# The sparse layer's mixer with projections written transposed

## The chip, the cores and the metric

One core of a Trainium2 chip runs the whole forward pass of a small two-layer trunk on 256 tokens of width 1024, batch 1, in float32. What counts is the device time of one execution in microseconds. A core has TensorE (PE), VectorE (DVE), ScalarE (ACT), GpSimd (POOL) and SyncE (SP), which here only issues transfers. Data lie in SBUF, TensorE writes PSUM, weights come from HBM.

## What is computed

Layer 0 has a mixer of a convolution and latent attention, layer 1 the sparse mixer that is changed here, and each has an MLP behind it. In the sparse mixer 16 heads in 4 groups look at keys in three ways: 15 compressed blocks, selected blocks (with 256 tokens all are selected, so it is causal attention with a slope) and a window. Gates weigh the three.

```python
proj = xn @ w_in          # q 1024 | k_c v_c k_s v_s k_w v_w, 256 each | gates 48
blk = z[:, idx] + pe      # 15 blocks of 32 tokens, starts 16 apart
kc = gelu(einsum('bnlgd,lde->bnge', blk_k, w1_k)) @ w2_k      # vc likewise
o_cmp = softmax(q kc' * scale - slope * dist) * has @ vc
o_slc = softmax(q k_s' * scale - slope * dist) @ v_s
o_win = softmax(q k_w' * scale - slope * dist) @ v_w
out = (g0 * o_cmp + g1 * o_slc + g2 * o_win) @ w_out
x = x + rms_norm(out, gain)
```

## The kernel before

Tokens are two tiles of 128 (`t`), the width is 8 slices of 128. Each product with weights is exact to nearly float32: weights and inputs are split into a high and a low part, and `mm3` (L112) adds three matmuls. A weight chunk (`chunk`, L156) is one transfer of 512 KB on SP into one of 4 raw buffers, two copies of 128x512 on ScalarE (`whi`) and two subtractions on VectorE (`wlo`); 5 slots hold them, 3 more (`x`) hold chunks that are loaded ahead for the next stage.

There are two forms of projection. Straight (`group_steps`, L202): the tokens are stationary and 512 (or 304, 256) weight columns move, tokens come out on partitions. Turned (`hidden_steps`, L346, in the MLPs): 128 weight columns are stationary and both token tiles move, 256 columns, outputs come out on partitions.

The order on TensorE is written out by hand. `mm` and `tr` add planned ns to a clock (`tick`), `defer(ns, fn)` puts a step off until the clock has passed, `need` runs steps until a condition holds, and `fill(ns)` in the head loop spends credit on pieces of other projections. The other engines' orders are made by the framework's scheduler from priorities.

The sparse mixer (`mixer_c`, L675) before: `c_in` group 0 (compressed inputs k_c, v_c) and group 1 (keys) straight, then v_s with gates, then queries of heads 0 to 7. What comes out on token rows is transposed by TensorE: tokens for the compression (`tok`, L650), split keys (L770), split queries (`q8`, L828). `compress` (L657) multiplies 16 slices onto 64 rows. In the head loop each of 32 head tiles has scores (`sc`) in two matmuls, then score reduction on VectorE (L921), exponential on ScalarE (L923), scaling by sum and gate on GpSimd (L928), and 5 heads later (`LAG`) a transposition of the probabilities (`pbn` to `pt`, L947). Eight heads make a unit; its compressed scores go through `cmp_scores` (`cs`, `cpc`, `ptc`), and its product with the values is given out piece by piece (`pv`). Remaining v_w, queries 8 to 15 and the output projection are the filling. `finish` (L275) ends a layer half: norm, update of X, transposition of the new X.

## Time and profile before

| | us |
|---|---|
| median of 3 runs (lowest, highest) | 645.55 (644.36, 645.79) |
| the profiled execution, its span | 644.01, 641.9 |
| TensorE, VectorE, ScalarE, GpSimd busy | 626.1, 418.2, 379.7, 78.0 |
| sparse mixer, first projection matmul to first MLP matmul | 307.37 to 454.87 |

Records of TensorE overlap, since matmuls are pipelined: 128x512 is shown with some 0.39 us though the next starts 0.23 us later. The price of an instruction is the time between starts, taken from a timeline, not its record.

### The profile page before, as it was taken

The page shows a single profiled execution, that of the slowest core. Times are in us where ns is not written, and L with a number is a line of the kernel's source. Part 1 is how long each engine was busy: PE and PEld are TensorE (multiplying, and loading weights), DVE is VectorE, ACT ScalarE, POOL GpSimd, SP SyncE. Part 2 cuts the span into 40 slices and gives each one's busy share as a digit, 9 for nine tenths or more (in the row PEclk, how much of TensorE's full clock was granted, in tenths as well). Part 3 has the DMA queues.
Part 4 walks back from the last instruction along what each step waited for, and adds up shares of the span by engine and source line. Part 5 has one row for each costly group of instructions (what it writes and reads, how often), then busy time and mean ns, then how long its engine had stood idle before and what let it go on. Part 6 is the DMA issues. An engine that isn't in the chain of part 4 may idle for free.

```text
span 641.9 us, 10332 instructions
## 1 busy us (share of the span) xinstructions
PE 626.1 (98%) x3630; PEld 532.5 (83%) x3630; DVE 418.2 (65%) x971; ACT 379.7 (59%) x866; POOL 78.0 (12%) x135
## 2 busy tenths in 40 slices
PE   7999999999999999999999999989999999999995
PEld 4889877889999988888889886666789999888884
DVE  6668797766666744446847787763966675644443
ACT  4886566756655644446727678875855565544431
POOL 1212330020000000000200055550300000000000
PEclk9999999999999999999999999999999999999999
DMA  8867335645555566556614825121646646556621
GB/s 270 293 184 219 124 106 198 222 138 196 192 178 188 185 205 198 194 185 244 213 34 136 290 99 165 33 67 58 210 149 209 198 166 201 191 197 195 197 68 65
DMA packets 32611, 110.09 MB, mean 172 GB/s; under 512 B 4080, under 2 KB 4656, under 8 KB 32560
## 3 DMA queue, kind: packets, MB, share of 16 engines
q1 hardware_dynamic: 32560, 109.44, 51.7%
q8 instruction: 28, 0.46, 0.3%
q14 instruction: 23, 0.19, 0.1%
HBM read 108.38 MB, written 1.05 MB: 170 GB/s over the span
## 4 chain that ended last, share of the span: by engine, by line
PE 63%; issue 28%; DVE 4%; ACT 2%; DMA 2%; POOL 1%; SPq 0%; DVEq 0%; POOLq 0%; ACTq 0%
PE acc L93 52%; PE sc L93 5%; PE tr L100 4%; DMA X<-in_x 1%; PE tr L105 1%; DMA raw<-in_a_in 1%; DVE wlo L172 1%; DVE xtl L255 1%; PE yp L93 1%; ACT pbn L923 1%; DVE X L293 1%; POOL rp L140 0%; ACT sq L270 0%; DVE xlo L172 0%; DVE pst L283 0%
## 5 line engine op out<-in xcount | busy, mean ns | idle before, releaser
L172 DVE TENSOR_TENSOR wlo<-raw,whi 128x512 fp32r<-128x512 f32 (+3 forms) x368 | 236.4, 681 | 123.3 <-ACT whi L171 121.3
L171 ACT ACTIVATE whi<-raw 128x512 fp32r<-128x512 f32 (+3 forms) x362 | 205.8, 614 | 135.5 <-PE acc L93 89.0
L93 PE MATMUL acc<-xtl,whi 128*128 128x256 f32 x384 | 107.9, 281 | 0.0
L93 PE MATMUL acc<-xth,wlo 128*128 128x256 f32 x384 | 107.5, 280 | 0.0
L93 PE MATMUL acc<-xth,whi 128*128 128x256 f32 x384 | 107.5, 280 | 0.0
L93 PE MATMUL acc<-whi,hl 128*128 128x512 f32 x256 | 99.8, 390 | 0.0
L93 PE MATMUL acc<-whi,hh 128*128 128x512 f32 x256 | 99.6, 389 | 0.0
L93 PE MATMUL acc<-wlo,hh 128*128 128x512 f32 x256 | 99.6, 389 | 0.0
L93 PE MATMUL acc<-whi,xth 128*128 128x512 f32 (+3 forms) x224 | 85.6, 382 | 1.1 <-DVE whi L167 1.1
L93 PE MATMUL acc<-wlo,xth 128*128 128x512 f32 (+3 forms) x224 | 84.4, 378 | 1.2 <-DVE wlo L172 1.0
L93 PE MATMUL acc<-whi,xtl 128*128 128x512 f32 (+3 forms) x224 | 85.2, 380 | 0.0
L93 PEld LDWEIGHTS acc<-xth,wlo 128*128 128x128 f32 x384 | 72.6, 189 | 0.0
L93 PEld LDWEIGHTS acc<-xth,whi 128*128 128x128 f32 x384 | 72.1, 188 | 0.1
L93 PEld LDWEIGHTS acc<-xtl,whi 128*128 128x128 f32 x384 | 72.1, 188 | 0.1
L93 PEld LDWEIGHTS acc<-whi,hh 128*128 128x128 f32 x256 | 48.1, 188 | 9.9
L93 PEld LDWEIGHTS acc<-wlo,hh 128*128 128x128 f32 x256 | 48.1, 188 | 9.9
L93 PEld LDWEIGHTS acc<-whi,hl 128*128 128x128 f32 x256 | 48.1, 188 | 9.9
L140 POOL TENSOR_TENSOR rp<-mse,mhalf 128x1 f32<-128x1 f32 x8 | 4.8, 596 | 395.4 <-DVE mse L137 395.4
L93 PEld LDWEIGHTS acc<-whi,xth 128*128 128x128 f32 x224 | 42.2, 188 | 10.3 <-issue 2.8
L93 PEld LDWEIGHTS acc<-wlo,xth 128*128 128x128 f32 x224 | 42.0, 188 | 8.8 <-DVE wlo L172 2.5
L93 PEld LDWEIGHTS acc<-whi,xtl 128*128 128x128 f32 x224 | 42.1, 188 | 6.6
L928 POOL TENSOR_SCALAR pbn<-pbn,sm,gates 128x128 f32<-128x128 f32 (+1 forms) x64 | 37.7, 600 | 75.1 <-DVE sm L925 72.7
(249 smaller groups left out, 883.4 us busy)
## 6 DMA issues: line engine op xcount, KB each, us to landing
raw<-in_w SPq DMA_DIRECT2D x128, 512.0 KB, 4.0
raw<-in_c_in SPq DMA_DIRECT2D x16, 512.0 KB, 3.7
raw<-in_a_in SPq DMA_DIRECT2D x15, 512.0 KB, 4.6
raw<-in_a_out SPq DMA_DIRECT2D x8, 512.0 KB, 3.7
raw<-in_c_out SPq DMA_DIRECT2D x8, 512.0 KB, 3.3
raw<-in_a_qup SPq DMA_DIRECT2D x6, 384.0 KB, 3.5
gpost<-in_gpost SPq DMA_DIRECT2D x4, 512.0 KB, 5.0
bias<-in_bias SPq DMA_DIRECT2D x4, 512.0 KB, 5.2
```

Of the source, the lines that this page charges most:

```text
L93: self.nc.tensor.matmul(ps, a, b, start=start, stop=stop, **({"skip_group_check": True} if part else {}))
L100: self.nc.tensor.transpose(dst, src, self.ident)
L105: self.nc.tensor.transpose(dst.bitcast(F32R), src, self.ident_r)
L140: nc.gpsimd.tensor_tensor(r, e, self.mhalf, op=OP.pow)
L171: nc.scalar.activation(hi[:, sl], raw[:, sl], AF.Copy)
L172: nc.vector.tensor_tensor(lo[:, sl], raw[:, sl], hi[:, sl].bitcast(F32), op=OP.subtract)
L255: nc.vector.scalar_tensor_tensor(lo, src, gcol, hi.bitcast(F32), OP.mult, OP.subtract)
L293: nc.vector.scalar_tensor_tensor(self.X[t][:, sl], self.tmp.pop(0), r, self.X[t][:, sl], OP.mult, OP.add)
L923: nc.scalar.activation(pb[:, sl], pb[:, sl], AF.Exp, bias=nm[:, br:br + 1], scale=-1.0, accum_out=sm[:, br:br + 1])
L928: nc.gpsimd.tensor_scalar(pb[:, sl], pb[:, sl], sm[:, br:br + 1], gates[t][:, 1 + br, h:h + 1], OP.mult, OP.mult)
```

## The change

Everything is in the sparse mixer and what leads into it; elsewhere the engines' orders stay.

- v_s with gates and v_w are projected first, straight (304 and 256 columns). The MLP before loads `c_v0` ahead instead of `c_in`.
- Keys, queries and compressed inputs are projected turned, in 4 groups of 96 matmuls of 128x256. The norm's factor lies along the columns then, so rx is turned into rows by two transpositions (`make_rows`), and the results are multiplied by them (`wide`). No transposition of keys, queries or tokens is left.
- Keys are wanted on both halves of the partitions: eight copies from SBUF to SBUF on SP bring the other half. The compression wants its input once more, one token later: two such copies (`epi_c`).
- `compress` has 8 matmuls onto 128 rows, two block halves at once; the upper rows are copied and added one block later.
- Compressed inputs and queries 8 to 15 are filling in the head loop, and so the compression itself runs there. Compressed scores come at heads 13, 16, 23 and 29; a unit's product with values comes in one block (`unit_pv`), the compressed part at its end (`unit_end`). `LAG` is 4, and the credits are given for each head.
- The output projection is filled in another order.

```diff
-LAG = 5
-PVN = (1, 1, 1, 1, 3, 3)
-FILL = (900.0, 1400.0, 1200.0, 800.0, 900.0, 1200.0, 900.0, 900.0, 1000.0, 1100.0, 1300.0, 1400.0)
+LAG = 4
+C_TILES = 2 * C_HEADS
+FILL = (1900.0,) * 6 + (1200.0,) * 10 + (300.0,) * 5 + (700.0,) * 11 + (1200.0,) * 8
...
         nc = self.nc
-        pt = self.trp()
-        for g in range(GRP):
-            self.tr(pt[:, g, :], tok[:, g, :])
-        nc.scalar.activation(z[0:64, 0:4, t * P:(t + 1) * P], pt[0:64], AF.Copy)
...
-        nc.vector.tensor_copy(z[64:128, 0:4, lo:(t + 1) * P - 1], pt[64:128, :, 1 - t:])
...
-        ph = pp.tile([P, 512], F32, name="sc", tag="sc", bufs=2)
-        for i in range(16):
-            self.mm(ph[0:64, 0:75], w1[:, i, :], z[:, :, 2 * i:2 * i + 225:16], i == 0, i == 15, 4)
...
+        for i in range(8):
+            self.mm(ps, w1[:, i, :], z[:, :, 2 * i:2 * i + 241:16], i == 0, i == 7, 4)
+        p5 = ps.rearrange("p (g n) -> p g n", g=5)
+        low = pool.tile([64, 6, 16], F32, name="ccs", tag="ccs", bufs=1)
+        nc.scalar.activation(low[:, 0:5], p5[64:128], AF.Copy)
+        x5 = pool.tile([64, 6, 16], F32, name="cct", tag="cct", bufs=1)
+        nc.vector.tensor_tensor(x5[:, 0:5, 0:15], p5[0:64, :, 0:15], low[:, 0:5, 1:16], op=OP.add)
...
+        nc.vector.tensor_scalar(xx, x5[:, 0:4, 0:15], x5[:, 4, 0:1], None, OP.add)
...
+    def mixer_c(self, x, rx, both, fin):
...
-                self.first_two(self.group_steps(x, "c_in", 0, 8, 512, epi_c, 0, cs=cs),
-                               self.group_steps(x, "c_in", 1, 8, 512, epi_k, 1))
-                self.group(x, "c_v0", 0, 8, 304, epi_v(0), 0)
-                self.need(lambda: left[0] == 10)
...
+                def later():
+                    pt = self.trp()
+                    for t in range(2):
+                        self.tr(pt[:, t, :], rxw[:, t])
+                    nc.scalar.activation(rows[0], pt[:, 0:2], AF.Copy)
+                    nc.scalar.activation(rows[1], pt[:, 0:2], AF.Copy, scale=0.125)
+                self.defer(1500.0, later)
...
+            vcs_ = self.chunks("c_v1", 0, range(2), 4, 256)
+            self.first_two(self.group_steps(x, "c_v0", 0, 8, 304, epi_v(0), 0, cs=self.ahead),
+                           self.group_steps(x, "c_v1", 0, 8, 256, epi_v(1), 1, k=4, cs=vcs_), 8)
...
+            def scaled(ps, i):
+                s = qp.tile([P, 2, 256], F32, name="sp", tag="pbn", bufs=6)
+                nc.vector.tensor_tensor(s, ps, wide(i), op=OP.mult)
+                return s
+
+            def epi_k(gp, ps):
+                s = scaled(ps, 0)
+                for par in range(2):
+                    rows_, other = slice(64 * par, 64 * par + 64), slice(64 - 64 * par, 128 - 64 * par)
+                    s_ = s[rows_].rearrange("p a (t n) -> p a t n", t=2)
+                    h, l = (m[rows_, 2 * gp + par] for m in (kTh, kTl))
+                    nc.scalar.activation(h, s_, AF.Copy)
+                    nc.vector.tensor_tensor(l, s_, h.bitcast(F32), op=OP.subtract)
+                    for m in (kTh, kTl):
+                        nc.sync.dma_start(m[other, 2 * gp + par].bitcast(F32), m[rows_, 2 * gp + par].bitcast(F32))
 
...
-                    def later(i):
-                        pt = self.trp()
-                        for r in range(4):
-                            self.tr_r(pt[:, r, :], q8[:, 4 * i + r, :])
...
+                def epi(b, ps):
+                    s = scaled(ps, 1)
+                    q = lp.tile([P, REP, 2, P], F32R, name="qT", tag="qT", bufs=3)
+
...
+                        h, l = (q[r, par:4:2] for r in (rows_, other))
                         with self.tc.high_priority():
...
+                            nc.scalar.activation(h, s_, AF.Copy)
+                            nc.vector.tensor_tensor(l, s_, h.bitcast(F32), op=OP.subtract)
+                    qT[2 * j + b] = q
+                    got.add(2 * j + b)
                 return epi
-            self.group(x, "c_in", 2, 8, 512, epi_q(0), 0)
...
+            def epi_c(i, ps):
+                with self.tc.high_priority():
+                    for par in range(2):
+                        rows_ = slice(64 * par, 64 * par + 64)
+                        nc.vector.tensor_tensor(z[i][0:64, par:4:2, :], ps[rows_], wide(0)[rows_], op=OP.mult)
+                    nc.sync.dma_start(z[i][64:128, 0:4, 0:S - 1], z[i][0:64, 0:4, 1:S])
+                self.defer(5500.0 + 2500.0 * i, lambda: fold(i))
...
+            def fold(i):
+                if i == 0:
+                    cps.append(self.acc(0))
+                    self.compress(qp, cps[0][:, 0:80], z[0], w1[0], "ck", out_k)
+                    self.defer(4500.0, last_k)
+                else:
+                    self.compress(qp, cps[0][:, 80:160], z[1], w1[1], "cv", out_v)
+                    self.defer(4500.0, last_v)
...
+            def last_v():
...
+                for a in range(2):
+                    self.mm(ph[:, a * 64:(a + 1) * 64], hv[:, 2 * a:2 * a + 2].rearrange("p b c n -> p (b c n)"),
+                            w2v, True, True, 4)
...
+            self.turned(both, "c_in", 1, epi_k)
+            for i, n in enumerate("kv"):
+                nc.sync.dma_start(w1[i], A["cw1_" + n])
+                nc.sync.dma_start(z[i][:, 4, :], A["pe_" + n])
+            nc.sync.dma_start(w2k, A["w2k"])
+            nc.sync.dma_start(w2v, A["w2v"])
+            self.turned(both, "c_in", 2, epi_q(0))
...
+            fills = [("c", always, self.turned_steps(both, "c_in", 0, epi_c)),
+                     ("q", always, self.turned_steps(both, "c_in", 3, epi_q(1))),
+                     ("o", mixed(0, 0), out_steps(0, 0, (0, 1))),
+                     ("o", mixed(1, 0), out_steps(0, 1, (0, 1))),
+                     ("o", mixed(1, 0), out_steps(1, 0, (0, 1))),
+                     ("o", mixed(1, 0, C_TILES), out_steps(1, 1, (0, 1))),
+                     ("p", mixed(0, 1), out_steps(0, 0, (2, 3))),
+                     ("p", mixed(0, 1), out_steps(1, 0, (2, 3))),
+                     ("r", mixed(1, 1), out_steps(0, 1, (2, 3))),
+                     ("r", mixed(1, 1), out_steps(1, 1, (2, 3)))]
...
+                    for b in range(2 * nb):
+                        br, kb = b // nb, b % nb
+                        for par in range(2):
+                            self.mm(y[64 * par:64 * par + 64, :],
+                                    vv[kb][:, br * 2 + gp, 64 * par:64 * par + 64],
+                                    pts[2 * gp + par, t][:, b].rearrange("p a b -> p (a b)"), b == 0, False, 2,
+                                    part=True)
...
+            def scores_c(gp, t):
+                self.need(lambda: left[0] == 2)
+                fns = self.cmp_scores(qp, pp, [q and q[:, :, t] for q in qT], kc, cbias[:, t], gates[t], gp, t, ptc)
+                self.defer(6000.0, fns[0])
...
+            at = {}
+            for u, i in enumerate((13, 16, 23, 29)):
+                at.setdefault(i, []).append(lambda u=u: scores_c(*units[u]))
+            for u in range(4):
+                at.setdefault(8 * u + 8 + LAG, []).append(lambda u=u: unit_pv(*units[u]))
+                at.setdefault(max(8 * u + 8 + LAG, 17), []).append(lambda u=u: unit_end(*units[u]))
...
+            fill(2200.0)
...
+                    if i == 16:
+                        force("q")
                     prob[i] = head_qk(*heads[i])
...
+                for fn in at.get(i, []):
+                    fn()
+                fill(FILL[i])
...
+            for cg in range(2):
+                for c in range(4):
+                    out_chunk(cg, c)
```

How the change moves instructions, at three places. TensorE where the transpositions of X1 (token tile 1 after layer 0) stand, before and then after; `acc0`, `acc1` are accumulators, `tr` is the PSUM tile of a transposition, `xth`, `xtl` the split input.

```order
L93 MATMUL acc0_3505<-xhi_3342,xth_3432 128x512
L93 MATMUL acc0_3505<-xlo_3343,xth_3432 128x512
L93 MATMUL acc0_3505<-xhi_3342,xtl_3433 128x512
L100 MATMUL tr_3533<-ident_70,X1_79 128x128 x4
L93 MATMUL acc0_3505<-whi_3350,xth_3432 128x512
L93 MATMUL acc0_3505<-wlo_3351,xth_3432 128x512
L100 MATMUL tr_3548<-ident_70,X1_79 128x128 x4
L93 MATMUL acc0_3505<-whi_3350,xtl_3433 128x512
```

```order
L92 MATMUL acc1_3553<-wlo_3499,xth_3413 128x256
L92 MATMUL acc1_3553<-whi_3498,xtl_3414 128x256
L99 MATMUL tr_3560<-ident_70,X1_79 128x128 x4
L92 MATMUL acc1_3553<-whi_3498,xth_3413 128x256
L92 MATMUL acc1_3553<-wlo_3499,xth_3413 128x256
L92 MATMUL acc1_3553<-whi_3498,xtl_3414 128x256
L92 MATMUL acc1_3553<-whi_3498,xth_3413 128x256
L99 MATMUL tr_3577<-ident_70,X1_79 128x128 x4
L92 MATMUL acc1_3553<-wlo_3499,xth_3413 128x256
L92 MATMUL acc1_3553<-whi_3498,xtl_3414 128x256
```

Ahead of the first one stand 18 matmuls of 512 columns of the sparse layer before, 24 of 304 and 6 of 256 after; two of 512 stood between the two transpositions, now four of 256.

TensorE at the end of the second unit (heads 12 to 20), before and then after; `pbn` are a head's probabilities, `kc` and `cpc` keys and split probabilities of the compressed part, `ptc` the latter turned, `pt` the former turned, `vcs` and `vv` values.

```order
L100 MATMUL tr_4518<-ident_70,pbn_4363 128x128 x4
L93 MATMUL sc_4524<-kTh_3473,qT_4131 128x512
L93 MATMUL sc_4524<-kTl_3474,qT_4131 128x512
L93 MATMUL acc1_4537<-ptc_4240,vcs_3479 128x512
L100 MATMUL tr_4539<-ident_70,pbn_4389 128x128 x4
L93 MATMUL sc_4545<-kTh_3473,qT_4131 128x512
L93 MATMUL sc_4545<-kTl_3474,qT_4131 128x512
L105 MATMUL tr_4548<-ident_r_71,q8_4514 128x128 x4
L93 MATMUL acc1_4537<-pt_4285,vv0_3475 64x512
L105 MATMUL tr_4566<-ident_r_71,q8_4514 128x128 x4
L93 MATMUL acc1_4537<-pt_4413,vv0_3475 64x512
L100 MATMUL tr_4574<-ident_70,pbn_4428 128x128 x4
```

```order
L99 MATMUL tr_4662<-ident_70,pbn_4500 128x128 x4
L92 MATMUL sc_4668<-kTh_3484,qT_4488 128x256
L92 MATMUL sc_4668<-kTl_3485,qT_4488 128x256
L104 MATMUL tr_4681<-ident_r_71,cpc_4575 128x128 x4
L92 MATMUL acc1_4510<-ptc_4686,vcs_3490 128x512
L99 MATMUL tr_4693<-ident_70,pbn_4544 128x128 x4
L92 MATMUL sc_4699<-kTh_3484,qT_4488 128x256
L92 MATMUL sc_4699<-kTl_3485,qT_4488 128x256
L99 MATMUL tr_4712<-ident_70,pbn_4587 128x128 x4
L92 MATMUL sc_4718<-kTh_3484,qT_4488 128x256
L92 MATMUL sc_4718<-kTl_3485,qT_4488 128x256
L99 MATMUL tr_4731<-ident_70,pbn_4606 128x128 x4
```

Between heads stood transpositions of queries and single products with values, now the transposition of the compressed probabilities and the end of the first unit's product.

ScalarE at the same place, before and then after; `whi` are weight copies, `qT` the split queries.

```order
L171 ACTIVATE whi_4999<-raw_4997 128x512
L171 ACTIVATE whi_5031<-raw_5029 128x512
L923 ACTIVATE pbn_4471,sm2_4473<-pbn_4471,nm2_4472 128x256 x2
L171 ACTIVATE whi_5031<-raw_5029 128x512
L1043 ACTIVATE ptc_4509<-tr_4504 128x512
L923 ACTIVATE pbn_4494,sm2_4496<-pbn_4494,nm2_4495 128x256
L947 ACTIVATE pt_4517<-tr_4518 128x4x128
```

```order
L768 ACTIVATE qT_4529<-sp_4527 64x2x256 x2
L937 ACTIVATE pt_4661<-tr_4662 128x4x128
L1026 ACTIVATE cpc_4575<-cs3_4563 128x16x16
L913 ACTIVATE pbn_4627,sm2_4629<-pbn_4627,nm2_4628 128x128 x2
L913 ACTIVATE pbn_4671,sm2_4673<-pbn_4671,nm2_4672 128x128 x2
L1035 ACTIVATE ptc_4686<-tr_4681 128x512
L1016 ACTIVATE cs3_4646<-cs3_4646 128x128
L961 ACTIVATE xth_4689<-acc1_4510 128x512
```

The copy of the turned compressed probabilities stood among weight copies and one head's exponentials; now it has the queries' high part, the split of the same probabilities and two heads' exponentials ahead of it.

## Rows read from the trace of the kernel before

**Rows 1.** The page, part 1: busy time of each engine (share of the span, number of instructions).

```profile
PE 626.1 (98%) x3630; PEld 532.5 (83%) x3630; DVE 418.2 (65%) x971; ACT 379.7 (59%) x866; POOL 78.0 (12%) x135
```

**Rows 2.** The timeline of TensorE (columns here and in all timelines: start in us from the span's start, us, engine, line, operation, output and inputs, shapes, count, and in brackets the idle time before it and what ended it). First the first matmul of the sparse layer's input projection, then the first of the MLP behind it.

```profile
307.37 0.40 PE L93 MATMUL acc<-xhi,xth 128*128 128x512 f32 x1
...
454.87 0.39 PE L93 MATMUL acc<-xhi,xth 128*128 128x512 f32 x1
```

**Rows 3.** The view by windows, two stretches of 20 us among the heads: the stretch and its us, then busy us and instructions of TensorE, its weight loads, VectorE, ScalarE and GpSimd, granted clock, DMA share, GB/s.

```profile
400.00:420.00 20.00, 18.73 (x108) 11.76 (x107) 16.43 (x84) 15.92 (x58) 10.04 (x20) 1.00 0.08 27
420.00:440.00 20.00, 18.91 (x98) 13.45 (x100) 9.23 (x34) 14.49 (x38) 8.44 (x12) 1.00 0.16 54
```

**Rows 4.** The waits of TensorE between 307 and 454 us: who waited, for whom, us in total, times, longest.

```profile
PE sc L93 <- DVE nm L921: 1.7, 1, 1.7
PE tr L105 <- DVE q L819: 1.3, 1, 1.3
PE tr L100 <- DVE X L293: 0.8, 1, 0.8
PE tr L105 <- ACT qT L828: 0.7, 1, 0.7
PE tr L100 <- ACT pt L947: 0.7, 1, 0.7
```

**Rows 5.** The timeline of TensorE where four split queries are transposed between the two halves of a score and three matmuls of the projection.

```profile
384.92 0.54 PE L105 MATMUL tr<-ident_r,q 128*128 128x128 f32 x4 [0.74 <-ACT qT L828]
...
385.60 0.39 PE L93 MATMUL acc<-whi,xth 128*128 128x512 f32 x1
385.83 0.40 PE L93 MATMUL acc<-wlo,xth 128*128 128x512 f32 x1
```

**Rows 6.** The timeline of TensorE in the first turned group of the MLP behind (256 columns moving), ten starts between the two rows; and from the page the loads of weights of such matmuls (busy us, mean ns).

```profile
499.75 0.28 PE L93 MATMUL acc<-xth,whi 128*128 128x256 f32 x1
...
500.92 0.28 PE L93 MATMUL acc<-xtl,whi 128*128 128x256 f32 x1
...
L93 PEld LDWEIGHTS acc<-xth,wlo 128*128 128x128 f32 x384 | 72.6, 189 | 0.0
```

**Rows 7.** The timeline of TensorE where four split keys are transposed.

```profile
338.23 0.45 PE L105 MATMUL tr<-ident_r,kdh 128*128 128x128 f32 x4
338.52 0.46 PE L93 MATMUL acc<-wlo,xth 128*128 128x512 f32 x1
```

**Rows 8.** The timeline of TensorE where four token blocks of the compression are transposed.

```profile
316.87 0.60 PE L100 MATMUL tr<-ident,tok 128*128 128x128 f32 x4
317.23 0.48 PE L93 MATMUL acc<-xlo,xth 128*128 128x512 f32 x1
```

**Rows 9.** The timeline of TensorE at the compression of keys and the start of that of values.

```profile
326.86 4.32 PE L93 MATMUL sc<-z_k,cw_k 128*64 128x75 f32 x32
331.00 1.08 PE L93 MATMUL sc<-z_v,cw_v 128*64 128x75 f32 x7
```

**Rows 10.** The timeline of TensorE at the compression's last product, 128 weight columns and 64 moving.

```profile
340.25 0.66 PE L93 MATMUL sc<-w2v,hv 64*128 64x64 f32 x4
340.84 0.53 PE L105 MATMUL tr<-ident_r,kdl 128*128 128x128 f32 x4
```

**Rows 11.** The timeline of TensorE at probabilities times values (each matmul is two records): the only block of four, and what comes next.

```profile
439.18 1.94 PE L93 MATMUL acc<-pt,vv 128*64 128x512 f32 x8
441.05 0.50 PE L93 MATMUL sc<-whi,xth 128*128 128x512 f32 x1
```

**Rows 12.** The group of probabilities times values between 307 and 454 us: count, then busy us and mean ns of one.

```profile
L93 PE MATMUL acc<-pt,vv 128*64 128x512 f32 x48 | 13.6, 613 | 0.0
```

**Rows 13.** The timelines around X1 before the sparse layer: TensorE's transposition, VectorE's update of X, GpSimd's rsqrt for the norms.

```profile
311.57 0.60 PE L100 MATMUL tr<-ident,X 128*128 128x128 f32 x4
...
309.99 1.42 DVE L293 SCALAR_TENSOR_TENSOR X<-pst,rp,X 128x512 f32<-128x512 f32 x2 [0.41 <-POOL rp L140]
...
311.61 2.73 POOL L140 TENSOR_TENSOR rx<-mse,mhalf 128x1 f32<-128x1 f32 x1 [1.66 <-DVE mse L137]
317.41 0.55 POOL L140 TENSOR_TENSOR rx<-mse,mhalf 128x1 f32<-128x1 f32 x1 [3.07 <-DVE rq L695]
```

**Rows 14.** Groups by form in the heads (365 to 450 us; GpSimd 300 to 465): ScalarE's exponential and copy, VectorE's score reduction, GpSimd's scaling of a head of the second token tile; busy us, mean ns.

```profile
L923 ACT ACTIVATE pbn<-pbn,nm 128x256 f32<-128x256 f32 x32 | 16.0, 502 | 6.6 <-DVE nm L921 4.8 <-POOL pbn L928 1.8
...
L947 ACT ACTIVATE pt<-tr 128x512 f32<-128x512 f32 x16 | 9.5, 593 | 5.2 <-PE tr L100 5.2
...
L921 DVE CUSTOM_DVE_ANT_0 pbn<-sc,bias 128x256 f32<-128x256 f32 x32 | 12.8, 415 | 1.3 <-PE sc L93 1.0
...
L928 POOL TENSOR_SCALAR pbn<-pbn,sm,gates 128x256 f32<-128x256 f32 x32 | 21.2, 673 | 14.8 <-DVE sm L925 12.4 <-ACT q L818 2.4
```

**Rows 15.** The timeline of TensorE at one head of the second token tile: transposition of an earlier head, then the two halves of the scores.

```profile
393.31 0.60 PE L100 MATMUL tr<-ident,pbn 128*128 128x128 f32 x4
393.67 0.48 PE L93 MATMUL sc<-kTh,qT 128*128 128x512 f32 x1
393.98 0.40 PE L93 MATMUL sc<-kTl,qT 128*128 128x512 f32 x1
```

**Rows 16.** DMA issues: what, engine, count, KB each, median us from issue to landing.

```profile
raw<-in_c_in SPq DMA_DIRECT2D x16, 512.0 KB, 3.7
...
out<-X SPq DMA_DIRECT2D x4, 256.0 KB, 2.0
```

315 lines of the change are left out of this document (107 added, 208 removed).

## The prediction

> **What bounds the kernel now.** I read the page first. TensorE is busy 98% of the span, VectorE and ScalarE 65% and 59% [rows 1], so time can only come out of TensorE's own stream or out of its gaps. The stage that the change rewrites runs from the first matmul of the sparse layer's input projection to the first of the next MLP's, 307.37 to 454.87 us [rows 2]. In two windows where the heads run TensorE is short of its 20 us by 1.3 and 1.1, and VectorE and ScalarE are 46 to 82% busy [rows 3]. The view of waits names five gaps of TensorE in the stage [rows 4], 5.2 us together; the starts of the instructions around them give 6.1, since a refill after a gap costs a little more than the gap. The reader should see that each of the five stands at an instruction of the sparse layer's own making (a transposition of split queries, a copy of probabilities, a score slot, the new X), not at a weight.
>
> For TensorE I take the time from one start to the next, since its records overlap. A straight matmul (512 columns moving) costs 0.23 us (385.60 to 385.83, [rows 5]), a turned one (256 moving) 1.17/10 = 0.117 [rows 6].
>
> **What is removed and added on TensorE.**
> Queries: 8 groups of four transpositions go. One group with the matmul behind it takes 0.68 us in place of 0.23 (384.92 to 385.60, [rows 5]), so 0.45 each: -3.6 us.
> Keys: 8 groups (hi and lo) go; their parts are the same form, one start to the next 0.29 [rows 7] and about 0.1 on the matmul behind: 0.40 each, -3.2 us.
> Tokens for the compression: 4 groups, 0.36 and the same 0.09 behind [rows 8]: -1.8 us.
> The same products are now 4 groups of 96 turned matmuls in place of 4 of 48 straight: 4 x (96 x 0.117 - 48 x 0.2325) = +0.3; I take +0.5. Two transpositions that turn rx into rows: +0.3.
> Compression: before, 32 records of 64 weight columns take 331.00 - 326.86 = 4.14 us [rows 9], 0.129 each, and there are two such runs (8.4 with the second). After, each has 8 matmuls onto 128 rows, 16 records. No row has this form. The nearest one above is the four records with 128 weight columns and 64 moving, 0.59/4 = 0.148 with what they cost behind them [rows 10]; the nearest below is the present 0.129 less the few columns. 32 records then cost 3.6 to 4.7; I take 4.2, near the present row, as the moving width is nearly unchanged: -4.2 us (-3.7 to -4.8).
> Probabilities times values: the 24 matmuls are now in blocks. Four in a block take 1.87 us [rows 11], so 24 x 0.4675 = 11.2 in place of the 12.8 that I sum from each start to the next over the 48 records (13.6 by the records themselves [rows 12]): -1.6 (0 to -2, since the block in the trace is a single one).
> Sum on TensorE: -3.6 - 3.2 - 1.8 + 0.8 - 4.2 - 1.6 = -13.6 us.
>
> On the compression the Trainium skill speaks against the change: "TensorE: Matmul & The Clock Gate", section "LDWEIGHTS (loading the stationary operand)", says that a weight load costs by its columns, not by its rows. Were the load what sets the pace, 16 records of 128 columns would cost what 32 of 64 cost, and the term would be 0 and not -4.2. The four records of 128 columns in rows 10 are nearly as cheap as those of 64 in rows 9, so the trace speaks against that; I keep it as a rival.
>
> **The old gaps.** All five go with their instructions, or are replanned: -6.1 us. What is late next is the question, so I walked the new order row by row with durations of this trace, each engine in its own order, each instruction starting when its engine is free and its inputs are there.
>
> **The new gaps.** (1) *X1.* Before, the first transposition of X1 came at 311.57 and its halves were updated from 309.99 to 311.41, some 0.9 us ahead of each transposition [rows 13]. Now the cover is 24 matmuls of 304 and 6 of 256 columns, 4.05 us by width in place of 18 x 0.2325 = 4.2, and the update is later, by some 1.9 in the walk: ScalarE has the two squares of X0 and a weight copy ahead of the square that it needs, and GpSimd has X0's rsqrt (rx) ahead of X1's (rp). 1.9 - 0.9 + 0.15 is 1.2; between +0 (as before) and +2.6 (rx in the way too) I take +1.5.
> GpSimd's rsqrt took 2.73 us beside a run of weight splits on VectorE, against 0.55 alone [rows 13]. The Trainium skill ("GPSIMD Engine Reference", section "1. Specifications") says why this may be: its SBUF interfaces are shared with VectorE, and instructions with two SBUF inputs contend. By that, rp would wait out the split that now stands ahead of X1's update, some 0.6 us more; without it nothing. Both lie within the bounds above.
> (2) *Heads 13 to 20.* This is the main term. Here the plan finds no filling work: the last query group is used up and the output projection has nothing mixed before the first unit ends (acc1_4510 with ptc_4686). Two sets of compressed scores come between, and the stretch from the transposition ahead of head 13 to the end of the second unit holds 14.4 us of TensorE work by the prices above. ScalarE's rows for the same heads sum to 14.8, VectorE's to 13.2. The prices: a head of the second token tile costs ScalarE two exponentials of 0.50 and a copy of 0.49, VectorE two score reductions of 0.34 and GpSimd two scalings of 0.54 from start to start, where the records are about 0.1 longer [rows 14]; TensorE needs 0.90 for it (0.36 + 0.31 + 0.23) [rows 15]. All three queues are equally long and feed each other, so a hand-over that is late is not made up. The walk stops TensorE at the scores of head 16 for 0.45 and at the second compressed scores behind them for 0.6; at the transposition of cpc_4575 for 2.3 (its split on VectorE stands behind the low half of the last queries, qT_4529); at the product with ptc_4686 for 1.15 (that copy stands behind four exponentials on ScalarE); from head 20's scores to the second unit's block for 0.8, and at its last product for 0.1: +5.4 us. If nothing lost step it would be the longest queue's 14.8 less 14.4, +0.4; if the waits ran two thirds longer, each behind one more neighbour, +9.
> (3) *Last unit.* Its product now stands right behind the last transposition; the copy on ScalarE (0.49 and the weight copy before it) is waited for: +0.5 (0 to 1).
> (4) *X0 at the end* was waited for 0.78 before [rows 4], and nothing in the new order gives it more cover: +0.8 (0 to 1.5). (5) Single hand-overs elsewhere: +0.5 (0 to 1).
> Sum: +8.7 us.
>
> **What costs nothing, and why.** The second halves of keys now come by eight copies from SBUF to SBUF, the shifted compression input by two, all on SP's queue. No row shows such a copy; the nearest are the write of X, 256 KB in 2.0 us, and a weight chunk of 512 KB, 3.7 [rows 16]. The keys have a whole query group to land in (96 x 0.117 = 11.2 us) plus the start of the next. The shifted input has 5.5 us of planned work before it is read, against two multiplications on VectorE (an estimate of 1.2 to 1.4: 512 columns each, where a score reduction of 256 takes 0.34 [rows 14]) and a copy of 2.0 to 3.7 behind a weight chunk's issue: 3.5 to 6.9 with the queue, so it is mostly covered; uncovered it costs up to 1.4 for each of the two, and more if weights queue behind. The compression's own chains have 4.5 us of planned cover against some 4.2 to 5.1.
>
> **Net.** -13.6 - 6.1 + 8.7 = -11.0 us. The profiled execution took 644.0 us, so 633.0 by its own time. The median of the runs is 645.55, 1.5 above it: 634.5.
>
> **Rivals.**
> *The thin stretch is hidden:* ScalarE and VectorE run ahead of TensorE, and (2) costs its floor of 0.4. Net -16.0: about 629.5. For it speaks that the plan keeps four heads between scores and transposition; against it that three engines have 13 to 15 us of work in the same 14.4.
> *A copy from SBUF to SBUF is late:* either the keys or the shifted input, with weight chunks behind it on SP's queue. The two compressions and the first compressed scores then stop TensorE for 1 to 5 us more: 636 to 640. For it: nothing in the trace shows such a copy, and the queue is in order.
> *The compression gains nothing* (the load sets its pace): +4.2, 638.7.
> *Slower: the turned matmul pays for its weights.* In the four groups every matmul has a new weight load of 0.19 us as recorded for half the moving columns. If the loads were not hidden there, each would cost 0.19 in place of 0.117, 384 x 0.071 = +27 us: 662. It decides from 11.0/384 = 0.029 us on, that is a matmul at 0.146. Against it: the MLP's turned matmuls, of the very same form, run at 0.117 [rows 6].
> *The change doesn't do what it says:* the order shows that the groups of transpositions are gone, so this can only be the plan's cover failing, case (2) at its worst: +3.6, 638.
>
> **How the numbers follow.** Forecast 634.5 with 630 to 638.5 for its own bounds: 0.62. Thin stretch hidden 0.12, a late copy 0.13, compression without gain 0.05, slower 0.08. The range 629 to 641 holds the first four but for tails, about 8 in 10. A measurement of this kernel tells 0.2% (1.3 us) from no change. Faster by more than that holds all but the slow case and the ends of the late copy: 0.89; same 0.03; slower 0.08.
>
> **What the new profile would show.** Right: no transpositions of queries, keys and tokens; turned matmuls of the projection at 0.117 from start to start; a compression run of 2.0 to 2.4 us; TensorE's waits in the stage 7 to 10 us, with most of it between the 13th and 20th head, on the transposition of the compressed probabilities. Wrong: waits of that stretch under 2 us or over 9, a wait on a DMA of z or kTh, or turned matmuls above 0.13.

## The result and the profile after

The kernel after takes 639.71 us (median of 4 runs, 638.87 to 640.04), the kernel before on the same chip 645.05 (644.36 to 645.79): ratio 0.9915, interval 0.9898 to 0.9932. The forecast was 634.5 with a range of 629 to 641: the direction and the range held, but the gain is 5.3 us in place of 11.0. The profiled execution took 639.43 us (span 637.6, mean granted clock 0.991) against 644.01 before (641.9, 0.998). All times and ratios here are of fast executions; of the experiment e6 two of six, at 1572 and 2307 us, are left out.

The page of the kernel after, busy times and granted clock by slices. TensorE is busy 8 us less than in [rows 1], and two slices of the clock row are an 8, the 25th, which is looked at below, and the last of the span:

```profile
PE 617.9 (97%) x3712; PEld 536.6 (84%) x3712; DVE 423.2 (66%) x975; ACT 375.0 (59%) x860; POOL 78.6 (12%) x135
...
PEclk9999999999999999999999998999999999999998
```

The timeline of TensorE, first matmul of the sparse layer's input projection, two turned matmuls fourteen starts apart, first matmul of the next MLP. The stage takes 143.57 us, against 147.50 in [rows 2]: -3.93. A turned matmul costs (361.39 - 359.76)/14 = 0.116 us, as in [rows 6].

```profile
307.18 0.30 PE L92 MATMUL acc<-xhi,xth 128*128 128x304 f32 x1
...
359.76 0.28 PE L92 MATMUL acc<-xth,whi 128*128 128x256 f32 x1
...
361.39 0.28 PE L92 MATMUL acc<-xth,wlo 128*128 128x256 f32 x1
...
450.75 0.40 PE L92 MATMUL acc<-xhi,xth 128*128 128x512 f32 x1
```

The waits of TensorE between 300 and 460 us. Of the five of [rows 4] those on transposed queries and on pt are gone, that on nm is shorter and at other heads, and X is waited for twice (X1 at the start, X0 at the end). With four new ones (cpc, z_k, ptc, cct) they sum to 9.4 us, against 5.2 before:

```profile
PE tr L99 <- DVE X L292: 2.7, 2, 1.7
PE tr L104 <- DVE cpc L1027: 2.4, 1, 2.4
PE acc L92 <- DMA z_k<-z_k: 2.0, 1, 2.0
PE sc L92 <- DVE nm L911: 0.9, 2, 0.6
PE acc L92 <- ACT ptc L1035: 0.7, 1, 0.7
PE acc L92 <- DVE cct L659: 0.7, 1, 0.7
```

*The shifted compression input.* The timelines of TensorE and of SP's queue, and the DMA issues (count, KB each, median us from issue to landing). TensorE stands from 362.0 to 364.0 ahead of the first compression, for a copy issued at 358.11. Four weight chunks of 512 KB were issued just ahead of it; the first two had landed, the third (issued at 354.31, 4.5 us) landed 0.7 us later, the fourth (issued at 356.80, 6.3 us) only at 363.1. The copy landed in 5.8 us. The compressions themselves are short: 2.19 and 2.09 us from start to start, 4.28 for 32 records, half of the 8.38 of the two runs that [rows 9] show in part.

```profile
363.99 2.46 PE L92 MATMUL acc<-z_k,cw 128*128 128x80 f32 x16 [1.99 <-DMA z_k<-z_k]
366.18 0.39 PE L92 MATMUL sc<-kTl,qT 128*128 128x256 f32 x1
...
369.35 2.37 PE L92 MATMUL acc<-z_v,cw 128*128 128x80 f32 x16
371.44 0.39 PE L92 MATMUL acc<-xth,whi 128*128 128x256 f32 x1
...
372.94 0.43 PE L92 MATMUL acc<-hk,w2k 64*128 64x60 f32 x2 [0.65 <-DVE cct L659]
...
350.63 6.49 SPq L159 DMA_DIRECT2D raw<-in_c_out  x4
358.11 0.65 SPq L779 DMA_DIRECT2D z_k<-z_k  x1
```

```profile
kTh<-kTh SPq DMA_DIRECT2D x4, 128.0 KB, 3.5
...
z_k<-z_k SPq DMA_DIRECT2D x1, 255.0 KB, 5.8
```

*Heads 13 to 20.* The timeline of TensorE, then VectorE and ScalarE around the compressed probabilities. The low part of cpc stands on VectorE behind the low part of the last queries (qT, 392.32), its high part on ScalarE behind two parts of qT and a copy of pt. TensorE stands 2.37 us. For the next three heads a transposition is recorded with 1.05 us in place of 0.60, and they come every 1.28 us.

```profile
394.68 0.75 PE L104 MATMUL tr<-ident_r,cpc 128*128 128x128 f32 x4 [2.37 <-DVE cpc L1027]
396.12 0.79 PE L92 MATMUL acc<-ptc,vcs 128*128 128x512 f32 x1 [0.69 <-ACT ptc L1035]
396.71 1.05 PE L99 MATMUL tr<-ident,pbn 128*128 128x128 f32 x4
...
397.99 1.05 PE L99 MATMUL tr<-ident,pbn 128*128 128x128 f32 x4
...
392.32 1.59 DVE L769 TENSOR_TENSOR qT<-sp,qT 64x512 fp32r<-64x512 f32 x2 [0.24 <-ACT qT L768]
...
394.21 0.42 DVE L1027 TENSOR_TENSOR cpc<-cs,cpc 128x256 fp32r<-128x256 f32 x1
...
391.67 1.27 ACT L768 ACTIVATE qT<-sp 64x512 fp32r<-64x512 f32 x2
392.96 0.60 ACT L937 ACTIVATE pt<-tr 128x512 f32<-128x512 f32 x1
393.59 0.42 ACT L1026 ACTIVATE cpc<-cs 128x256 fp32r<-128x256 f32 x1
```

The windows of the same stretch (columns as in [rows 3]) say why. TensorE is busy 1.07 of 4 us from 392 to 396, and in the next window the granted clock is 0.50, the lower of its two levels (1.2 in place of 2.4 GHz). TensorE is then full, VectorE and ScalarE are not.

```profile
388.00:392.00 4.00, 3.28 (x26) 2.77 (x24) 3.97 (x23) 4.00 (x16) 1.96 (x3) 1.00 0.32 92
392.00:396.00 4.00, 1.07 (x7) 0.67 (x5) 3.50 (x13) 3.93 (x13) 3.09 (x5) 0.79 0.65 220
396.00:400.00 4.00, 3.88 (x18) 3.70 (x18) 2.92 (x15) 2.40 (x7) 1.39 (x4) 0.50 0.03 6
```

*Probabilities times values.* The timeline at two blocks. The block of eight matmuls (16 records) takes 4.61 us, the block of four 2.38, against 1.87 in [rows 11]. (The trace before has two such blocks of four and not only one; the second, from 442.64 on, takes 1.87 too.)

```profile
418.62 2.45 PE L92 MATMUL acc<-pt,vv 128*64 128x512 f32 x8
421.00 0.50 PE L92 MATMUL acc<-ptc,vcs 128*128 128x512 f32 x1
...
435.39 4.68 PE L92 MATMUL sc<-pt,vv 128*64 128x512 f32 x16
440.00 0.50 PE L92 MATMUL sc<-ptc,vcs 128*128 128x512 f32 x1
```

*X1.* The timelines of TensorE, VectorE, GpSimd and ScalarE, and at the end ScalarE's in the kernel before. The last cover starts at 311.12, X1's transposition at 313.11. On ScalarE the square that X1's update needs (sq of acc and r) stands behind the two squares of X0 (sq of X); before, it came ahead of them. rp was done by 311.81; VectorE had taken a weight split first (after waiting 0.52 us for its high part) and then updated X from 312.31.

```profile
311.12 0.28 PE L92 MATMUL acc<-whi,xtl 128*128 128x256 f32 x1
313.11 0.65 PE L99 MATMUL tr<-ident,X 128*128 128x128 f32 x4 [1.71 <-DVE X L292]
...
311.70 0.69 DVE L171 TENSOR_TENSOR wlo<-raw,whi 128x512 fp32r<-128x512 f32 x1 [0.52 <-ACT whi L170]
312.31 1.41 DVE L292 SCALAR_TENSOR_TENSOR X<-pst,rp,X 128x512 f32<-128x512 f32 x2
...
309.28 1.52 POOL L139 TENSOR_TENSOR rx<-mse,mhalf 128x1 f32<-128x1 f32 x1 [5.78 <-DVE mse L136]
311.26 0.55 POOL L139 TENSOR_TENSOR rp<-mse,mhalf 128x1 f32<-128x1 f32 x1 [0.45 <-DVE mse L136]
...
306.78 0.65 ACT L269 ACTIVATE sq<-X 128x512 f32<-128x512 f32 x1
...
307.92 0.64 ACT L269 ACTIVATE sq<-X 128x512 f32<-128x512 f32 x1
...
309.05 0.69 ACT L284 ACTIVATE sq<-acc,r 128x512 f32<-128x512 f32 x1
```

```profile
307.63 0.69 ACT L285 ACTIVATE sq<-acc,r 128x512 f32<-128x512 f32 x1
```

### The profile page after: what moved, and what is told of

It is laid out like the page before. It is cut to its first block, busy times and chain, and to the rows that moved or that the text cites. A ratio compares the mean times of both kernels' runs of the same rounds, so it can differ in the third digit from the quotient of the medians.

```text
span 637.6 us, 10525 instructions
## 1 busy us (share of the span) xinstructions
PE 617.9 (97%) x3712; PEld 536.6 (84%) x3712; DVE 423.2 (66%) x975; ACT 375.0 (59%) x860; POOL 78.6 (12%) x135
## 3 DMA queue, kind: packets, MB, share of 16 engines
HBM read 108.38 MB, written 1.05 MB: 172 GB/s over the span
## 4 chain that ended last, share of the span: by engine, by line
PE 60%; issue 28%; DVE 6%; ACT 2%; DMA 2%; POOL 1%; SPq 0%; DVEq 0%; POOLq 0%; ACTq 0%
PE acc L92 52%; PE sc L92 4%; PE tr L99 4%; DVE wlo L171 2%; ACT pbn L913 1%; DMA raw<-in_a_in 1%; DMA z_k<-z_k 1%; DVE xtl L254 1%; PE yp L92 1%; DVE X L292 1%; POOL rp L139 0%; DVE xlo L171 0%; DVE pst L282 0%; DVE pbn L911 0%; POOL rx L139 0%
## 5 line engine op out<-in xcount | busy, mean ns | idle before, releaser
L92 PE MATMUL acc<-xtl,whi 128*128 128x256 f32 x512 | 143.8, 281 | 0.0
L92 PE MATMUL acc<-xth,whi 128*128 128x256 f32 x512 | 143.5, 280 | 0.0
L92 PE MATMUL acc<-xth,wlo 128*128 128x256 f32 x512 | 143.5, 280 | 0.0
L92 PEld LDWEIGHTS acc<-xth,whi 128*128 128x128 f32 x512 | 96.3, 188 | 1.0 <-issue 0.8
L92 PEld LDWEIGHTS acc<-xth,wlo 128*128 128x128 f32 x512 | 96.7, 189 | 0.1
L92 PEld LDWEIGHTS acc<-xtl,whi 128*128 128x128 f32 x512 | 96.2, 188 | 0.2
L92 PE MATMUL acc<-wlo,xth 128*128 128x512 f32 (+3 forms) x160 | 60.3, 379 | 1.3 <-DVE wlo L171 1.1
L92 PE MATMUL acc<-whi,xth 128*128 128x512 f32 (+3 forms) x160 | 60.3, 377 | 0.7 <-DVE whi L166 0.7
L92 PE MATMUL acc<-whi,xtl 128*128 128x512 f32 (+3 forms) x160 | 60.5, 378 | 0.0
L92 PEld LDWEIGHTS acc<-whi,xth 128*128 128x128 f32 x160 | 30.2, 189 | 5.6 <-ACT xth L252 1.1
```

What stands on the lines that cost most here:

```text
L92: self.nc.tensor.matmul(ps, a, b, start=start, stop=stop, **({"skip_group_check": True} if part else {}))
```

## The experiments

My theory: the missing half of the gain lies in four places that add up, namely the late shifted input (2.2 us by starts), the stop at cpc with the clock that falls behind it, X1, and the broken blocks of probabilities times values. The rival: VectorE and ScalarE are the bound of the head stretch, and the other waits are covered again further on, so that mending one moves the time elsewhere. The profiled executions differ by up to 2.7 us in where the stage begins (307.1 to 309.8), since in three of them (e3, e5, e10) the granted clock also falls between 8 and 20 us, and a span is that of one execution; so lengths inside the stage are compared beside spans and medians. The sections used, with their lengths in the kernel after: stage start to first scores 40.69; first scores to head 8 25.42; head 8 to 12 7.23; head 12 to 21 26.56; head 21 to 31 18.68; head 31 to the MLP 24.99.

**e1_warm: keep TensorE at work through the stop.** Nine matmuls on zeros go into the tile that the transposition of the first unit's cpc then overwrites.

```diff
+            for _ in range(9 if (gp, t) == (0, 0) else 0):
+                nc.tensor.matmul(pt.rearrange("p a b -> p (a b)"), self.wm[:, 0:P], self.wm, start=True, stop=True)
             for r in range(REP):
...
+        self.wm = warm
```

> The changed kernel with nine matmuls of zeros (128x512, bfloat16, some 0.21 us each) put on TensorE into the PSUM tile of the transposition just ahead of the transposition of the first unit's compressed probabilities, where TensorE stood idle for 2.37 us and after which its granted clock was 0.5 for some 6.5 us. They only take up idle time; the transpositions overwrite them. Theory A (the idle time costs twice: itself, and then the lower clock): the wait on cpc shrinks to under 0.7 us by the view of waits, the granted clock between 394 and 402 us stays at 1.0, the three heads behind come every 0.75 to 0.9 us and not every 1.28, and the span falls by 1.8 to 2.6 us. Theory B (VectorE and ScalarE set the pace there, the clock only fills idle time): the clock stays up but the waits come back at the heads behind, and the span falls by less than 0.7.

Measured: 640.53 us (637.9 to 641.65), ratio 0.9918 [0.9886, 0.995]; span 636.1. By time alone it is not told from the kernel after. The profiled execution is the fastest of four; the others have a mean clock of 0.993 to 0.996 in place of 0.998 and take 1.6 to 3.8 us longer, and no trace shows where their clock fell. Inside the profiled one, head 12 to 21 takes 25.14 (-1.4) and the span is 1.5 shorter, between the two expectations; the clock is 1.00 in every window of the stage, and the heads behind the stop are recorded at 0.60 again (of the nine matmuls the trace has eight):

```profile
391.88 2.12 PE L1032 MATMUL tr<-wm 128*128 128x512 bf16 x8
394.41 0.53 PE L104 MATMUL tr<-ident_r,cpc 128*128 128x128 f32 x4 [0.41 <-DVE cpc L1027]
...
396.14 0.60 PE L99 MATMUL tr<-ident,pbn 128*128 128x128 f32 x4
```

cpc comes no earlier, so what is saved inside is the price of the lower clock alone; e7 repeats it on a better base.

**e2_zact: the shifted input by ScalarE.**

```diff
-                    nc.sync.dma_start(z[i][64:128, 0:4, 0:S - 1], z[i][0:64, 0:4, 1:S])
+                    nc.scalar.activation(z[i][64:128, 0:4, 0:S - 1], z[i][0:64, 0:4, 1:S], AF.Copy)
```

> The changed kernel with the shifted half of the compression's input written by ScalarE (two copies of 64 partitions x 1020 elements) in place of the two copies from SBUF to SBUF on SP's queue. Theory A (the copy's own 5.8 us to landing are what TensorE waits for): the wait on z_k, 2.0 us, is gone, the compression starts within 0.3 us of its place in the order, and the span falls by 1.5 to 2.2 us. Theory B (what follows in the compression's chain is late anyway, or ScalarE's two copies of about 1.1 us push back the exponentials): the wait moves to the next product of the chain or to the scores, and the span falls by less than 0.7.

Measured: 637.88 us (636.41 to 638.32), ratio 0.9879 [0.9857, 0.9901]; span 636.1. The wait on z is gone, and first scores to head 8 falls from 25.42 to 23.19: -2.2, as theory A has it. Nothing grows behind it (head 12 to 21 26.61). The wait was a real one and not covered again.

**e3_norm: the norms' squares of X0 as late as the other layers'.**

```diff
-        self.defer(3000.0 if idx == 2 else 8000.0, norm)
+        self.defer(8000.0, norm)
```

> The changed kernel with one part of the change undone: X0's norm before the sparse layer is put off by 8000 planned ns again and not 3000, so that on ScalarE its two squares no longer stand ahead of the square that X1's update needs, and on GpSimd rx of X0 stands behind rp of X1. Theory A (this order is what makes X1 late): the wait on X1 falls from 1.71 to under 0.7 us and the span by 1.0 to 1.7. Theory B (the narrower v projections in front give too little cover, whatever the order): the wait stays above 1.2.

Measured: 636.17 us (635.78 to 636.75), ratio 0.9857 [0.9837, 0.9877]; span 634.9. X1's wait is gone (stage start to first scores 38.77, -1.92), as theory A has it. Unlooked for, z's wait went too (first scores to head 8 23.19), and head 12 to 21 is 0.8 shorter, which is not explained. SP's queue and the DMA issues show how z gained: three weight chunks stand ahead of it in place of four, the last of them lands 0.6 us behind z's issue, and z lands in 3.0 us in place of 5.8.

```profile
350.88 4.07 SPq L159 DMA_DIRECT2D raw<-in_c_out  x3
358.55 0.65 SPq L779 DMA_DIRECT2D z_k<-z_k  x1
```

```profile
z_k<-z_k SPq DMA_DIRECT2D x1, 255.0 KB, 3.0
```

**e10_zq: the same copies, issued by GpSimd.** Is it the order on SP's queue, or the chunks in flight?

```diff
-                    nc.sync.dma_start(z[i][64:128, 0:4, 0:S - 1], z[i][0:64, 0:4, 1:S])
+                    nc.gpsimd.dma_start(z[i][64:128, 0:4, 0:S - 1], z[i][0:64, 0:4, 1:S])
```

> The changed kernel with only the two shifted copies of the compression's input issued by GpSimd and not by SP, so that they no longer stand behind the fourth weight chunk of the output projection on SP's queue, though the chunk's bytes are still under way at the same time. Theory A (the copy waits its turn in SP's queue behind that chunk): it lands in 3 to 3.6 us, as in the run where the chunk stood behind it, and the wait on z_k falls from 2.0 to under 0.5 us. Theory B (the chunks in flight share the DMA engines with it, whatever the queue): it lands in over 4.5 us and the wait stays above 1.2.

Measured: 639.17 us (638.41 to 643.85), ratio 0.9925 [0.9904, 0.9946]. The profiled execution is one of the two slowest, at 643.85. In it z still lands in 5.2 us, beside a chunk issued 1.6 us ahead that takes 5.8, and the first compression waits 1.6 us, as theory B has it. Another queue does not help here. With e3 it points at the chunk in flight; what a copy issued by GpSimd costs with nothing beside it, no run shows. Behind this wait of 1.6 us the granted clock fell (0.95 and 0.62 in the windows of 4 us from 364 to 372), which it had not done behind 1.99 in the kernel after.

```profile
z_k<-z_k POOLq DMA_DIRECT2D x1, 255.0 KB, 5.2
```

**e5_sched: the first compressed scores two turns earlier, and filling work for heads 16 to 20.** The three numbers belong to the order of the heads: the turn of the compressed scores, the earliest turn of a unit's end, and the filling work planned for the last turns.

```diff
-FILL = (1900.0,) * 6 + (1200.0,) * 10 + (300.0,) * 5 + (700.0,) * 11 + (1200.0,) * 8
+FILL = (1900.0,) * 6 + (1200.0,) * 10 + (700.0,) * 5 + (700.0,) * 11 + (1200.0,) * 8
...
-            for u, i in enumerate((13, 16, 23, 29)):
+            for u, i in enumerate((11, 16, 23, 29)):
...
-                at.setdefault(max(8 * u + 8 + LAG, 17), []).append(lambda u=u: unit_end(*units[u]))
+                at.setdefault(max(8 * u + 8 + LAG, 16), []).append(lambda u=u: unit_end(*units[u]))
```

> The changed kernel with the first unit's compressed scores two head turns earlier (turn 11 and not 13), its end at turn 16 and not 17, and a credit of 700 ns and not 300 for turns 16 to 20; nothing else. Theory A (the stretch of heads 13 to 20 lacks work on TensorE while a long chain of the compressed probabilities is waited for): the wait on cpc falls from 2.4 to under 1 us, the granted clock there stays at 1.0, and the span falls by 3 to 6 us. Theory B (ScalarE and VectorE together are the bound of the stretch): the waits only move, and the span falls by less than 1.5.

Measured: 638.24 us (637.32 to 640.77), ratio 0.9882 [0.9858, 0.9905]; span 638.7 (the slowest of the five executions; its stage begins 2.5 us later and is 1.4 shorter). It came as neither theory has it. Head 12 to 21 is 2.45 shorter and head 8 to 12 0.9 longer, with the clock at 1.00, though the transpositions of cpc still wait 2.3 us; but here the clock fell behind the wait on z (2.1 us; 0.56 and 0.59 in 368 to 372), and first scores to head 8 grew by 1.5. Without z's wait it has to be tried again: e8.

**e6_four: what is mended, together.** The edits of e2 and e3; the products of the last unit one turn later; and cpc's two parts ahead of queued work.

```diff
-                at.setdefault(8 * u + 8 + LAG, []).append(lambda u=u: unit_pv(*units[u]))
-                at.setdefault(max(8 * u + 8 + LAG, 17), []).append(lambda u=u: unit_end(*units[u]))
+                at.setdefault(8 * u + 8 + LAG + u // 3, []).append(lambda u=u: unit_pv(*units[u]))
+                at.setdefault(max(8 * u + 8 + LAG + u // 3, 17), []).append(lambda u=u: unit_end(*units[u]))
...
-        nc.scalar.activation(pc[:, :, 0:4:2, :], wide, AF.Copy)
-        nc.vector.tensor_tensor(pc[:, :, 1:4:2, :], wide, pc[:, :, 0:4:2, :].bitcast(F32), op=OP.subtract)
+        with self.tc.high_priority():
+            nc.scalar.activation(pc[:, :, 0:4:2, :], wide, AF.Copy)
+            nc.vector.tensor_tensor(pc[:, :, 1:4:2, :], wide, pc[:, :, 0:4:2, :].bitcast(F32), op=OP.subtract)
```

> Four edits of the changed kernel together, each in its own part of the stage, so that each is read from its own stretch: X0's norm put off by 8000 again; the shifted compression input by ScalarE and not by a copy on SP; the last unit's product with values one turn later, so that a piece of the output projection stands between the last transposition and it; the split of the compressed probabilities at high priority in the scheduler. Theory A: gains add. From the stage's start to the first scores 38.8 us (40.7 in the changed kernel), from there to head 8's scores 23.2 (25.4), head 12 to head 21 25.0 to 25.9 (26.6, since the split comes some 0.8 us earlier), the last unit's eight products 3.7 to 3.9 (4.6) since they pair again; the span 5.5 to 7 us below the changed kernel's 637.6. Theory B (the waits are one another's cover, so that a gap closed in front opens one behind): less than 3.5.

Measured: 634.01 us (633.5 to 634.22), ratio 0.982 [0.9799, 0.9841]; span 632.4. The stage is 5.34 shorter than in the kernel after: X1 1.92, z 2.23, head 31 to the MLP 1.17. Three of the four gains add, as theory A has it; the span falls by 5.2, just short of its 5.5, because the fourth is missing. The last unit's block is whole again, 3.77 us in place of 4.61. The priority brought nothing that shows: cpc is still waited for 2.1 us (2.4), the clock falls again, and head 12 to 21 is as long as before.

```profile
432.33 3.84 PE L92 MATMUL sc<-pt,vv 128*64 128x512 f32 x16
436.10 0.50 PE L92 MATMUL sc<-ptc,vcs 128*128 128x512 f32 x1
```

```profile
388.00:392.00 4.00, 1.21 (x9) 0.81 (x7) 3.61 (x14) 3.85 (x13) 2.73 (x5) 0.83 0.70 231
392.00:396.00 4.00, 4.00 (x18) 3.82 (x19) 2.68 (x15) 2.54 (x8) 1.72 (x4) 0.50 0.02 4
```

**e7_five: e6 with e1's matmuls on zeros.**

> The four edits and the nine matmuls of zeros ahead of the first unit's compressed probabilities. Theory A (the clock's fall there costs time of its own): the granted clock stays at 1.0 in heads 13 to 21, head 12 to head 21 takes 1.2 to 2 us less than in the kernel with the four edits. Theory B (VectorE and ScalarE are the bound once the clock is up): within 0.6 us of it.

Measured: 632.36 us (632.13 to 632.86), ratio 0.9796 [0.9775, 0.9817]; span 630.8. Head 12 to 21 takes 24.43 in place of 26.55: 2.1 us, a little over theory A's 1.2 to 2, with the clock at 1.00 throughout the stage. All four executions are faster than the fastest of e6 (633.5). It has the lowest median here; e8 is not told from it.

```profile
388.00:392.00 4.00, 3.29 (x20) 1.79 (x19) 3.65 (x13) 3.85 (x13) 2.73 (x4) 1.00 0.80 240
```

**e8_sched: e5's order on e6's base** (without the priority).

> Norm, shifted input and last unit as in the four edits, and in place of the high priority the earlier compressed scores (first unit at turn 11, end at 16, credit of 700 ns in turns 16 to 20). Theory A (in the first try of this schedule the waits of the stretch fell, but a fall of the clock behind the wait on the shifted input took it back; without that wait the gain stays): head 8 to head 21 takes 30.5 to 32.3 us (33.8 in the changed kernel), the clock stays at 1.0 from 360 us on, and the span is 6.5 to 8.5 us below 637.6. Theory B (ScalarE bounds the stretch): head 8 to head 21 above 32.5.

Measured: 632.89 us (632.45 to 634.42), ratio 0.9812 [0.9789, 0.9835]; span 630.8. Head 8 to 21 takes 32.23 us, 33.79 in the kernel after, and the span is 6.8 shorter, as theory A has it. In the profiled execution the clock stays at 1.00, though the waits at the transpositions of cpc still sum to 2.3 us (1.8 and 0.5); two of the five executions have a mean clock of 0.992 in place of 0.998 and take 1.2 us and more longer. ScalarE is busy 4.00 of 4 us in two of the windows from 384 to 396. The stage is 1.0 shorter than in e7 (135.19 against 136.21) at the same span: in the MLP behind, TensorE now waits 1.0 us for a weight split (xlo), so there the time did move elsewhere.

**e11_pool: e8 with one chunk's high part on GpSimd,** to take two copies of some 0.6 us from ScalarE's full queue.

```diff
-                    out_cs[cg, c] = self.chunk(A["c_out"][cg, c], 2, 512)
+                    out_cs[cg, c] = self.chunk(A["c_out"][cg, c], 2, 512, pool_hi=(cg, c) == (0, 2))
```

> The kernel with the earlier compressed scores, the norm, the shifted input by ScalarE and the last unit one turn later, and one thing more: the high part of the weight chunk that is converted among heads 13 to 20 (output projection, first half, third chunk) is made by GpSimd, two instructions of 128x512, and not by ScalarE. Theory A (ScalarE, busy 4.0 of 4.0 us from 384 to 388 and from 392 to 396 there, sets the pace of the stretch): head 8 to head 21 falls from 32.2 to 30.8 to 31.6 us. Theory B (the chain through VectorE sets it, or GpSimd's own scalings are pushed back): within 0.4 us of 32.2 or above.

Measured: 633.4 us (632.25 to 635.08), ratio 0.9836 [0.9819, 0.9852]; span 630.3. No change, as theory B has it: head 8 to 21 32.20, and cpc's waits are 2.4 in place of 2.3.

**e9_lag: five heads between scores and transposition in place of four,** with e2, e3 and the last unit's edit.

```diff
-LAG = 4
+LAG = 5
...
-FILL = (1900.0,) * 6 + (1200.0,) * 10 + (300.0,) * 5 + (700.0,) * 11 + (1200.0,) * 8
+FILL = (1900.0,) * 6 + (1200.0,) * 10 + (300.0,) * 5 + (700.0,) * 11 + (1200.0,) * 9
```

> Norm, shifted input and last unit as in the four edits, and one more part of the change undone: five heads and not four between scores and transposition (LAG 5). Theory A (the distance is not what the stretch lacks, since its waits are on the compressed probabilities and not on a head's own): head 12 to head 21 within 0.8 us of the changed kernel's 26.6, span 4.5 to 6 us below 637.6. Theory B (four heads are too few, each head's chain is waited for): head 12 to head 21 falls by more than 1.5 us.

Measured: 639.77 us (639.0 to 640.8), ratio 0.991 [0.989, 0.993]; span 637.2: neither theory. The stage is 143.18 against e6's 138.23. Waits on score maxima come to 2.7 us in three places (e6 0.9 in two), 1.4 is waited for with no releaser named, and the clock is low for longer (0.69, 0.50 and 0.53 in the windows from 388 to 400, and once more 0.57 from 420 to 424). That cpc is waited for only 1.1 us does not help. Head 12 to 21 falls to 22.87, which theory B asked for, but the sections in front of and behind it hold other work now (head 8 to 12 11.65, head 21 to 31 26.93) and the span is no shorter; so the sections cannot be compared, and which of these comes first stays open.

## Why the prediction held in direction and missed half of the gain

**What the prediction's own signs said.** The turned matmuls at 0.116, the compression runs of 2.19 and 2.09 us and the 9.4 us of waits came as it said. But of these 9.4 only 4.0 lie among heads 13 to 20 (nm 0.9, cpc 2.4, ptc 0.7), which is not most of them, and one of its signs of being wrong came true: a wait on the transfer of z. The time lies outside the 630 to 638.5 that the forecast gave itself; it is inside 629 to 641 only because that was drawn around the rivals too. What was right is the list of terms on TensorE and the place of the longest stop; that the range held owes something to luck.

**TensorE's work.** The turned matmuls cost nearly what was said: 384 of them take 45.73 us, 0.119 each, 0.6 more than the sum allowed, mostly where one stands behind another form. So the rival in which they pay for their weights is out. The compression fell from 8.38 to 4.28: -4.1 for -4.2. The Trainium skill's rule ("TensorE: Matmul & The Clock Gate", section "LDWEIGHTS (loading the stationary operand)") is that a load costs by its columns, and the recorded loads agree: 0.153 us with 64 columns, 0.206 with 128. Had the load set the pace, there would have been no gain; but a record with 128 weight columns takes 0.134 us from start to start and one with 64 took 0.129 [rows 9], so the load did not set this pace.

**Probabilities times values: the term that changed its sign.** From each start to the next the stage's 24 products took 12.81 us before and take 13.76 now: +0.95 for -1.6. The step took the price of an undisturbed block [rows 11] for all. Two products onto the two halves of the output run side by side: before, one alone took 1.00 us and two together 1.01; in a block a pair takes some 0.95. The four blocks now take 1.98, 4.78, 2.38 and 4.61, in place of 1.87 and 3.74. In the second unit the transposition of the second unit's cpc stands inside the block, and the last product behind it is alone and takes 1.00. In the last unit the copy of its second head is late, the pairs break, and the block costs 4.61; e6, where that copy has a turn more, has 3.77. The forecast's +0.5 for that copy was the right place, but it is the pairing that pays.

**"What costs nothing" failed for the shifted input.** Its landing was bounded by 2.0 to 3.7 us from the write of X and a weight chunk [rows 16]; it took 5.8, and it is a wait of 2.2 us by starts. e2 shows that this is its whole price; e3 and e10 point at the chunk in flight as what makes it late. The rival of a late copy named it, at 0.13. The keys' copies landed in 3.5 us and cost nothing, as said. The compression's own chain added 1.0 (0.81 at w2k, 0.23 at hv) where the cover was called equal to it.

**Heads 13 to 20: mechanism right, size some 6.2 for 5.4.** The walk put 2.3 us on cpc behind the low part of the last queries: it is 2.37, behind that very instruction. The stops up to it, by starts, are 0.6, 0.4, 0.8 and 2.5, 4.2 together. What the term lacked is the clock: a stop was counted as its length, and behind this one the clock is halved for the heads that follow. By e7 against e6 the fall costs 2.1 us (e1 against the kernel after: 1.4). From the transposition ahead of head 13 (384.67) to the end of the second unit (406.26) 21.6 us pass: 7.2 more than the prediction's 14.4 of work, of which 1.05 are the second unit's products, counted above. And 14.4 is too much: the five heads of the first token tile cost 0.67 where the clock is up (e7, 392.58 to 393.25) and not 0.90, some 1.2 us less together, so that stops and clock come to some 7.3. The rival that VectorE and ScalarE are the bound of the stretch fits what is left in e8, where taking work from ScalarE alone (e11) changed nothing, but not the 2 us of the clock; that the two set what is left is not shown.

**X1 +1.87 for +1.5, X0 +1.19 for +0.8.** The cause of X1's is the one that the prediction gave, the order on ScalarE. From the stage's start X1's update comes 2.5 us later than before: the square that it needs 1.6 later, behind the two squares of X0, and two weight splits that VectorE takes first (309.71 and 311.70) some 0.45 each. e3 moves the two squares, and with nothing else done the update is back at 2.6 us from the start, as before; it gains 1.92. GpSimd was not in the way: rp took 0.55 us. rx took 1.52 beside splits on VectorE. The Trainium skill ("GPSIMD Engine Reference", section "1. Specifications") says that GpSimd shares its SBUF interfaces with VectorE and contends with instructions that have two SBUF inputs, as the splits do; 1.52 against 0.55 agrees, but it cost nothing here.

**The sum.** The stage is 3.93 us shorter; the other 0.65 of the profiled 4.58 came outside it, where nothing was forecast. Of the 7.1 us between -11.0 and -3.93: z 2.2, probabilities times values 2.55, the compression's chain 1.0, heads 0.75, turned matmuls 0.6, X1 0.4, X0 0.4, less 1.0 that stood in the forecast for the last unit and for single hand-overs: 6.9. With the heads' work at its lower price it is some 8.0, so the list closes to about a microsecond and no better. (The forecast's median lay 1.5 above the profiled time; here it lies 0.3 above.) z, X1, the last unit and the clock are shown by experiments; the rest of the products' price (the blocks of the first three units) and the compression's chain are read from rows only.
